# Order of the scores, transposes and gate products in the chunked RWKV pass of a hybrid decoder layer

## The chip, the cores and the metric

The kernel runs on 1 core of one Trainium2 chip. The metric is the device time of one execution in microseconds (us). A core has five engines that work side by side, each through its own queue in order: TensorE (PE: matmuls and transposes; PEld is its weight load), VectorE (DVE), ScalarE (ACT), GpSimd (POOL) and SyncE (SP), the last mostly for DMAs. TensorE writes to PSUM, in banks of up to 128 x 512 fp32 as this kernel uses them.

## The reference, cut to what matters

One layer: an input projection, then an RWKV-7 branch (16 heads of 64) beside an RG-LRU branch, a gated merge, cross-attention and an MLP, for one prompt of 512 rows and 8 single-row samples. The change touches the RWKV scan, which the kernel computes in chunks, and the gates of the RG-LRU:

```
def step(s, inp):                          # RWKV-7, for each row
    r_t, w_t, k_t, v_t, a_t, b_t = inp
    sa = jnp.einsum('bhvk,bhk->bhv', s, a_t)
    s = s * w_t[:, :, None, :] + sa[..., None] * b_t[:, :, None, :] + v_t[..., None] * k_t[:, :, None, :]
    y = jnp.einsum('bhvk,bhk->bhv', s, r_t)
    return s, y
...
gr = jax.nn.sigmoid(jnp.einsum('btnd,nde->btne', blk, W['lru_wa'][l]).reshape(xc.shape) + W['lru_ba'][l])
gi = jax.nn.sigmoid(jnp.einsum('btnd,nde->btne', blk, W['lru_wx'][l]).reshape(xc.shape) + W['lru_bx'][l])
```

## The kernel before, in words

The span begins with weight units: each loads a block of 128 columns of a projection, splits it into a high and a low part (wh by a ScalarE cast, line 95, wl by a VectorE subtraction, line 98), and multiplies it with the split input (xH, xL) into a pair of PSUM banks called mm. adv(n) records the next n units. These matmuls, some 48 a unit, are the filler of everything below.

The RWKV part runs in four passes J = 0 to 3 of two column blocks j = 2J, 2J + 1 (two heads each). For each j, stages E1 to E3 prepare r, k, v, the decays, and the chunk operands: ar (a and r, scaled by the decay up to the row) and bk (b and k, scaled back), eight chunks of 64 rows. Then stage_C1(j) (from line 656) makes

- the scores: 16 products bk x ar, for 8 chunks in two halves, each half into two banks (one a head), which VectorE multiplies with a mask into the tile SC (line 675);
- POOL's scaling of ar (line 678), and a memset of UV (line 682);
- BK: 8 transposes of bk into two banks, copied by ScalarE (line 688);
- UV: 4 transposes of v into one bank, copied by ScalarE (line 693);
- kp (line 697), a product of kp with a matrix of ones, and bv from it (line 701).

Banks: ps1() takes one of two banks (tile ps), psc(s) one of two single banks (tile ch), ps4() changes between both. After the second call stage_C2(J) inverts 32 x 32 triangles of SC on VectorE: two transposes into Am (line 712), a copy Tm, 30 pairs of small steps (tmp line 718, Tm line 720), transposes back (lines 724, 727), and then block products Am x SC and SC x Am on TensorE with ScalarE copies (lines 735, 744). In pass 3 the units of the inverse are mixed with the next work. stage_chain(J) then goes through the eight chunks; each step is a chain of TensorE product, ScalarE copy XS (line 771), product, VectorE copy UV (line 778), product, VectorE update, ScalarE copy y (line 806). Its steps are recorded between the units' matmuls.

gates() (line 541) is recorded behind a unit of the RG-LRU: 4 products of xc with block-diagonal weights bdw (lines 545, 546) into two mm pairs, two tanh each (547, 548), then a chain of activations (552, 553, 559, 560) and VectorE steps.

Around the end of pass 3 three other things are recorded: u_lru loads rows back from DRAM (POOL's DMA rw<-lin_d, line 1078, into two buffers), casts them to xH (ScalarE, line 1080) and xL (VectorE, line 1081); mem_rows transposes the memory tokens (tile mt) and splits them into mh (ScalarE, line 1113) and ml (VectorE, line 1114) for the attention's keys and values; and the u_G units write gate tiles gt (lines 574 to 576).

The order on each engine is drawn by a scheduler from the recorded program. Only a matmul or transpose recorded inside pinned() is tied to stand behind the one recorded before it, without a semaphore.

Of the kernel before, what the change touches and what calls it, by code (L numbers as in the profile page):

```python
# [8 lines left out]
F32 = mybir.dt.float32  # L9
F32R = mybir.dt.float32r  # L10
AF = mybir.ActivationFunctionType
OP = mybir.AluOpType
# [24 lines left out]
def build(tc, d, dbg=None):  # L37
# [43 lines left out]
    def ps4():  # L81

        nr4[0] += 1
        return ps1() if nr4[0] % 2 else psc(nr4[0] // 2 % 2)
# [420 lines left out]
    def u_L(i):  # L505
        def run_y(w):

            p = mm_full(w, X)
            ya, yb = et("ya", pool=LR), et("yb", pool=LR)
            ACT.copy(v2(yb), p[:, :, 0:HA])  # L510
            ACT.copy(SY[:, i, :], p[:, 1, HA:HB])
            ACT.activation(ya, yb, AF.Square, scale=GC)
            DVE.scalar_tensor_tensor(ya, ya, 1.0, yb, op0=OP.add, op1=OP.mult)
            ACT.activation(ya, ya, AF.Tanh, scale=GS)
            DVE.scalar_tensor_tensor(ya, ya, 1.0, yb, op0=OP.add, op1=OP.mult)
            lru[i] = ya
        wunit("w_in", NSH + D + i * 128, run_y)

        def run_u(w):
            ya = lru.pop(i)  # L520
            p = mm_full(w, X)
            ut, bd = ut_[i % 2], bdw[i % 2]
            for n, nm in enumerate(("lru_wa", "lru_wx")):
                for h in range(2):
                    hs = slice(64 * h, 64 * h + 64)
                    SP.dma_start(out=bd[hs, n, hs], in_=d[nm][0, 2 * i + h])
            xt_ = LR.tile([128, T], F32, tag="xc", name="xc")
            xc = xt_[:, 0:S]
            ACT.copy(v2(ut[:, 3:S + 3]), p[:, :, 0:HA])  # L529
            ACT.activation(v2(xc), p[:, :, 0:HA], AF.Identity, scale=par("conv_w", 24 + i),  # L530
                           bias=par("lru_conv_b", i))
            ACT.copy(SU[:, i, :], p[:, 1, HA:HB])
            POOL.tensor_copy(COUT[:, 0, :, i], ut[:, S:S + 3])  # L533
            DVE.tensor_scalar(xt_[:, S:T], SU[:, i, :], par("conv_w", 24 + i), par("lru_conv_b", i),
                              op0=OP.mult, op1=OP.add)
            for jj in range(3):
                cw = par("conv_w", 8 * jj + i)
                DVE.scalar_tensor_tensor(xc, ut[:, jj:jj + S], cw, xc, op0=OP.mult, op1=OP.add)
                DVE.scalar_tensor_tensor(xt_[:, S:T], CB[:, :, jj, i], cw, xt_[:, S:T], op0=OP.mult, op1=OP.add)
            POOL.tensor_copy(SX[:, i, :], xt_[:, S:T])  # L540
            def gates():
                tr, ti = et("tr", pool=LR), et("ti", pool=LR)
                for n, (o, so, bb) in enumerate(((tr, SR, hba), (ti, SI, hbx))):
                    p = mmps()
                    PE.matmul(p[:, 0, 0:HA], bd[:, n, :], xt_[:, 0:HA], start=True, stop=True)
                    PE.matmul(p[:, 1, 0:HB], bd[:, n, :], xt_[:, HA:T], start=True, stop=True)
                    ACT.activation(v2(o), p[:, :, 0:HA], AF.Tanh, scale=0.5, bias=bb[:, i:i + 1])
                    ACT.activation(so[:, i, :], p[:, 1, HA:HB], AF.Tanh, scale=0.5, bias=bb[:, i:i + 1])
                    yield
                DVE.scalar_tensor_tensor(xc, ti, 1.0, xc, op0=OP.add, op1=OP.mult)  # L550
                a0 = et("a0", pool=LR)
                ACT.activation(a0, tr, AF.Exp, scale=c4[:, i:i + 1], bias=c4[:, i:i + 1])
                ACT.activation(tr, tr, AF.Tanh, scale=c4h[:, i:i + 1], bias=c4h[:, i:i + 1])
                yield
                DVE.scalar_tensor_tensor(tr, a0, 1.0, tr, op0=OP.add, op1=OP.mult)
                DVE.tensor_scalar(a0, tr, -1.0, 1.0, op0=OP.mult, op1=OP.add)
                DVE.scalar_tensor_tensor(tr, a0, 1.0, tr, op0=OP.add, op1=OP.mult)
                yield
                ACT.activation(tr, tr, AF.Ln, bias=tiny)
                ACT.activation(tr, tr, AF.Exp, scale=0.5)  # L560
                DVE.scalar_tensor_tensor(xc, xc, 0.5, tr, op0=OP.mult, op1=OP.mult)
                DVE.tensor_tensor_scan(ti, a0, xc, 0.0, op0=OP.mult, op1=OP.add)
                yield
                POOL.tensor_copy(HOUT[:, 0, i:i + 1], ti[:, S - 1:S])
                DVE.scalar_tensor_tensor(ya, ya, 0.5, ti, op0=OP.mult, op1=OP.mult)
                POOL.dma_start(out=lin_d[i], in_=ya)
            later(lambda: side["queue"].append(gates()))
        wunit("w_in", NSH + i * 128, run_u)

# [86 lines left out]
    def stage_C1(j):  # L656
# [5 lines left out]
        SC = CJ["SC"]  # L662
        ar, bk, v = q["ar"], q["bk"], q["v"]
        scv = SC[:, 16 * s:16 * s + 16, :].rearrange("p (c h) n -> p h c n", h=2)
        for half in range(2):
            pp = [ps4(), ps4()]
            for c4_ in range(4):
                c = 4 * half + c4_
                for h in range(2):
# [3 lines left out]
            for h in range(2):  # L673
                p = pp[h]
                DVE.tensor_tensor(scv[:, h, 4 * half:4 * half + 4, :],
                                  p.rearrange("p (c n) -> p c n", c=4),
                                  mask.unsqueeze(1).to_broadcast([128, 4, 128]), op=OP.mult)
        POOL.tensor_tensor(ar[:, 1:NC_].rearrange("p c a t -> p c (a t)"), ar[:, 1:NC_].rearrange("p c a t -> p c (a t)"),
                           q["DL"][:, 0:NC_ - 1].unsqueeze(2).to_broadcast([128, NC_ - 1, 2 * C]), op=OP.mult)
        BK = Cp.tile([128, NC_, 128], F32, tag=f"BK{s}", name="BK")  # L680
        UV = Cp.tile([128, NC_, 128], F32, tag=f"UV{s}", name="UV")
        POOL.memset(UV[0:64], 0.0)
        for half in range(2):
            p = ps1()
            for c4_ in range(4):
                c = 4 * half + c4_
                PE.transpose(p[:, c4_ * 128:(c4_ + 1) * 128], bk[:, c].rearrange("p a t -> p (a t)"), ident)
            ACT.copy(BK[:, 4 * half:4 * half + 4].rearrange("p c n -> p (c n)"), p)
        p = ps1()
        for n in range(4):  # L690
            PE.transpose(p[:, n * 128:(n + 1) * 128], v[:, n * 128:(n + 1) * 128], ident)
        for h in range(2):
            ACT.copy(UV[64:128].rearrange("p (n h) m -> p h n m", h=2)[:, h],
                     p[64 * h:64 * h + 64].rearrange("p (n m) -> p n m", n=4))

        kp = q["kp"]
        DVE.scalar_tensor_tensor(kp, q["r"], par("rw_r_k", j), kp, op0=OP.mult, op1=OP.mult)
        p = ps1()
        PE.matmul(p, bd1, kp, start=True, stop=True)
        bv = et("bv", pool=EO)  # L700
        DVE.tensor_tensor(bv, p, v, op=OP.mult)
        q.update(SC=SC, BK=BK, UV=UV, bv=bv)
# [1268 lines left out]
```

## Time and profile before

| | us |
|---|---|
| median of 3 runs (lowest, highest) | 1376.09 (1371.07, 1384.85) |
| the profiled execution | 1376.98 |
| its span in the trace | 1375.2 |
| TensorE busy | 1295.8 (94%) |
| VectorE busy | 973.4 (71%) |
| ScalarE busy | 622.3 (45%) |
| GpSimd busy | 359.3 (26%) |

The span is from the first to the last instruction; 1.8 us of the execution lie around it. The mean granted TensorE clock over the span is 0.97 of full speed. Matmul ends are modelled, so TensorE's waits are best read from the brackets at the end of a row, which give the idle time before it and what ended it.

### The profile page before, as it was taken

The page shows a single profiled execution, that of the slowest core. Times are in us where ns is not written, and L with a number is a line of the kernel's source. Part 1 is how long each engine was busy: PE and PEld are TensorE (multiplying, and loading weights), DVE is VectorE, ACT ScalarE, POOL GpSimd, SP SyncE. Part 2 cuts the span into 40 slices and gives each one's busy share as a digit, 9 for nine tenths or more (in the row PEclk, how much of TensorE's full clock was granted, in tenths as well). Part 3 has the DMA queues.
Part 4 walks back from the last instruction along what each step waited for, and adds up shares of the span by engine and source line. Part 5 has one row for each costly group of instructions (what it writes and reads, how often), then busy time and mean ns, then how long its engine had stood idle before and what let it go on. Part 6 is the DMA issues. An engine that isn't in the chain of part 4 may idle for free. (4 is left out here: it accounts for less than half of the span.)

```text
span 1375.2 us, 27588 instructions
## 1 busy us (share of the span) xinstructions
PE 1295.8 (94%) x11098; PEld 1202.6 (87%) x11098; DVE 973.4 (71%) x1920; ACT 622.3 (45%) x1199; POOL 359.3 (26%) x423
## 2 busy tenths in 40 slices
PE   7997999999999999888899998998999999999996
PEld 7996988798878887787879998866999999999996
DVE  5578967797679875787855545665667777777755
ACT  4475476537653765443154234442454333333321
POOL 6311000200020012215423124252111444434312
PEclk9999999999999998798999999999999999999998
DMA  7422322221222132474549545784333333333311
GB/s 205 136 73 64 116 60 67 94 82 50 75 91 70 48 93 83 120 210 136 175 138 286 172 115 174 214 267 150 94 91 91 109 93 108 93 92 94 107 64 62
DMA packets 205973, 160.30 MB, mean 117 GB/s; under 512 B 12429, under 2 KB 190911, under 8 KB 205334
## 3 DMA queue, kind: packets, MB, share of 16 engines
q1 hardware_dynamic: 182502, 104.36, 26.1%
q0 software_dynamic: 14592, 47.80, 10.4%
q10 hardware_dynamic: 8752, 6.39, 1.5%
q8 instruction: 87, 1.43, 0.4%
q14 instruction: 40, 0.33, 0.1%
HBM read 137.11 MB, written 21.40 MB: 115 GB/s over the span
## 5 line engine op out<-in xcount | busy, mean ns | idle before, releaser
L47 PE MATMUL mm<-xH,wh 128*128 128x260 f32 (+2 forms) x1824 | 480.0, 292 | 5.9 <-DVE ff L1797 1.7
L47 PE MATMUL mm<-xL,wh 128*128 128x256 f32 (+2 forms) x1824 | 475.2, 289 | 1.0 <-DVE ff L1799 1.0
L47 PE MATMUL mm<-xH,wl 128*128 128x264 f32 (+2 forms) x1568 | 453.8, 290 | 1.2 <-DVE wl L98 1.2
L47 PEld LDWEIGHTS mm<-xH,wh 128*128 128x128 f32 x1824 | 329.9, 191 | 16.5 <-issue 4.3
L47 PEld LDWEIGHTS mm<-xL,wh 128*128 128x128 f32 x1824 | 329.7, 190 | 8.2 <-issue 4.7
L47 PEld LDWEIGHTS mm<-xH,wl 128*128 128x128 f32 x1568 | 298.8, 191 | 8.0 <-issue 4.0
L95 ACT CAST wh<-wr 128x1024 fp32r<-128x1024 f32 x120 | 125.2, 1053 | 178.7 <-PE mm L47 127.0
L47 PE MATMUL mm<-hl,wh 128*128 128x260 f32 (+2 forms) x1056 | 197.0, 285 | 0.9 <-ACT hl L1453 0.9
L98 DVE TENSOR_TENSOR wl<-wr,wh 128x1024 fp32r<-128x1024 f32 x120 | 151.9, 1271 | 56.1 <-ACT wh L95 55.5
L47 PEld LDWEIGHTS mm<-hl,wh 128*128 128x128 f32 x1056 | 163.8, 188 | 2.3 <-ACT hl L1453 1.0
L47 PE MATMUL mm<-hl,wl 128*128 128x260 f32 (+2 forms) x528 | 150.8, 286 | 0.0
L1631 DVE TENSOR_TENSOR wl<-wr,wh 128x512 fp32r<-128x512 f32 x104 | 92.7, 897 | 13.7 <-ACT wh L1630 13.3
L47 PEld LDWEIGHTS mm<-hl,wl 128*128 128x128 f32 x528 | 99.6, 189 | 0.6 <-issue 0.5
L1630 ACT CAST wh<-wr 128x512 fp32r<-128x512 f32 x104 | 62.3, 620 | 53.1 <-PE mm L47 36.4
L47 PE MATMUL mm<-xL,wl 128*128 128x260 f32 (+2 forms) x256 | 72.5, 283 | 0.0
L1799 DVE TENSOR_TENSOR ff<-ff,mm 128x520 f32<-128x520 f32 (+2 forms) x64 | 40.0, 626 | 40.1 <-PE mm L47 40.1
L533 POOL COPY OUTC<-ut 128x3 f32<-128x3 f32 x8 | 2.9, 366 | 193.0 <-ACT ut L529 193.0
L1631 DVE TENSOR_TENSOR wl<-ws,wh 128x512 fp32r<-128x512 f32 x48 | 39.2, 817 | 13.3 <-ACT wh L1630 13.1
L47 PEld LDWEIGHTS mm<-xL,wl 128*128 128x128 f32 x256 | 48.2, 188 | 0.0
L720 DVE TENSOR_TENSOR Tm<-Tm,tmp 64x30 f32<-64x30 f32 (+14 forms) x120 | 40.5, 338 | 3.4
L47 PE MATMUL mm<-mh,wh 128*128 128x256 f32 x128 | 38.8, 305 | 3.7 <-ACT ft L1129 1.8
L794 DVE SCALAR_TENSOR_TENSOR Sbd<-Sbd,DL,ch 64x64 f32<-64x64 f32 x112 | 31.4, 280 | 15.1 <-PE ch L47 12.4
(524 smaller groups left out, 2540.2 us busy)
## 6 DMA issues: line engine op xcount, KB each, us to landing
wr<-in_w_in_dram SPq DMA_DIRECT2D x58, 512.0 KB
wr<-in_mlp_up_dram SPq DMA_DIRECT2D x32, 512.0 KB
wr<-in_mlp_down_dram SPq DMA_DIRECT2D x32, 512.0 KB
vc<-in_cache_mem_v_dram POOLq DMA_DIRECT2D x32, 256.0 KB, 7.3
ff<-in_cache_mem_k_dram POOLq DMA_DIRECT2D x32, 256.0 KB, 4.0
gat_d<-gt POOLq DMA_DIRECT2D x16, 260.0 KB, 2.7
wr<-in_xa_wk_dram SPq DMA_DIRECT2D x8, 512.0 KB
wr<-in_xa_wv_dram SPq DMA_DIRECT2D x8, 512.0 KB
```

The source lines that it names most:

```text
L47: r = nc.tensor.matmul(*a, **k)
L95: a = ACT.copy(h, raw)
L98: DVE.tensor_tensor(l, raw, h.bitcast(F32), op=OP.subtract)
L533: POOL.tensor_copy(COUT[:, 0, :, i], ut[:, S:S + 3])
L720: DVE.tensor_tensor(Tm[:, i + 1:32, 0:i], Tm[:, i + 1:32, 0:i], tv, op=OP.add)
L794: DVE.scalar_tensor_tensor(Sn[s][hs, hs], So[s][hs, hs], Q[s]["DL"][hs, c - 1:c], PX[hs, cs], op0=OP.mult, op1=OP.add)
L1630: pin(ACT.copy(h, src))
L1631: pin(DVE.tensor_tensor(l, src, h.bitcast(F32), op=OP.subtract))
L1799: DVE.tensor_tensor(z, z, p, op=OP.add)
```

## The change

stage_C1 makes UV's memset and kp first. Then, pinned in this order on TensorE: the 8 transposes of bk (ps1, both banks) with the BK copies, the first half of the scores into psc(0) and psc(1), the 4 transposes of v with the UV copies, the product for kp, and the second half of the scores into the same two banks. POOL's scaling of ar and bv follow. The gates' four products are pinned as well. The instructions are the same ones, in number and size.

```diff
                 for n, (o, so, bb) in enumerate(((tr, SR, hba), (ti, SI, hbx))):
                     p = mmps()
-                    PE.matmul(p[:, 0, 0:HA], bd[:, n, :], xt_[:, 0:HA], start=True, stop=True)
-                    PE.matmul(p[:, 1, 0:HB], bd[:, n, :], xt_[:, HA:T], start=True, stop=True)
+                    with pinned():
+                        PE.matmul(p[:, 0, 0:HA], bd[:, n, :], xt_[:, 0:HA], start=True, stop=True)
+                        PE.matmul(p[:, 1, 0:HB], bd[:, n, :], xt_[:, HA:T], start=True, stop=True)
...
-        for half in range(2):
-            pp = [ps4(), ps4()]
+        BK = Cp.tile([128, NC_, 128], F32, tag=f"BK{s}", name="BK")
+        UV = Cp.tile([128, NC_, 128], F32, tag=f"UV{s}", name="UV")
+        POOL.memset(UV[0:64], 0.0)
+
+        kp = q["kp"]
+        DVE.scalar_tensor_tensor(kp, q["r"], par("rw_r_k", j), kp, op0=OP.mult, op1=OP.mult)
+
+        def scores(half):
+            pp = [psc(0), psc(1)]
             for c4_ in range(4):
...
+        with pinned():
+            for half in range(2):
+                p = ps1()
+                for c4_ in range(4):
+                    c = 4 * half + c4_
+                    PE.transpose(p[:, c4_ * 128:(c4_ + 1) * 128], bk[:, c].rearrange("p a t -> p (a t)"), ident)
+                ACT.copy(BK[:, 4 * half:4 * half + 4].rearrange("p c n -> p (c n)"), p)
+            scores(0)
+            p = ps1()
+            for n in range(4):
+                PE.transpose(p[:, n * 128:(n + 1) * 128], v[:, n * 128:(n + 1) * 128], ident)
...
+            p = ps1()
+            PE.matmul(p, bd1, kp, start=True, stop=True)
+            scores(1)
         POOL.tensor_tensor(ar[:, 1:NC_].rearrange("p c a t -> p c (a t)"), ar[:, 1:NC_].rearrange("p c a t -> p c (a t)"),
                            q["DL"][:, 0:NC_ - 1].unsqueeze(2).to_broadcast([128, NC_ - 1, 2 * C]), op=OP.mult)
-        BK = Cp.tile([128, NC_, 128], F32, tag=f"BK{s}", name="BK")
...
```

(The lines removed behind the last one are the same transposes, copies, kp and product in their old place.)

Where the scheduler then puts things is shown at three places. From line 545 on, line numbers of the changed kernel are about one higher, in stage_C1 up to 26 off, and some six higher behind it.

First, TensorE at the first call of stage_C1 in pass 0. Before, from the last scores on (ch and ps are banks, xc,bdw the gates' products, ident,bk the transposes of bk):

```order
L47 MATMUL ch<-ar,bk 128x128
L47 MATMUL ps<-ar,bk 128x128
L47 MATMUL mm<-xc,bdw_277 128x256 x2
L47 MATMUL mm<-xc,bdw_277 128x264 x2
L47 MATMUL mm<-xH,wh 128x256
L47 MATMUL mm<-xL,wh 128x256
L47 MATMUL mm<-xH,wl 128x256
L47 MATMUL mm<-xH,wh 128x256
L52 MATMUL ps<-ident,bk 128x128 x4
```

and in the changed kernel:

```order
L47 MATMUL mm<-xc,bdw_277 128x256
L47 MATMUL mm<-xc,bdw_277 128x264
L47 MATMUL mm<-xc,bdw_277 128x256
L47 MATMUL mm<-xc,bdw_277 128x264
L52 MATMUL ps<-ident,bk 128x128 x8
L47 MATMUL ch<-ar,bk 128x128 x8
L52 MATMUL ps<-ident,v_668 128x128 x4
L47 MATMUL ps<-kp,bd_102 128x512
L47 MATMUL ch<-ar,bk 128x128 x8
L47 MATMUL mm<-xH,wh 128x256
```

The 16 scores have gone from ahead of the gates' products to behind them, and no mm product stands between the parts of stage_C1.

Second, ScalarE at the start of the chain in pass 2 (SC the last block products' copies, XS and y the chain's copies, sq and ic activations of the next pass's decays, ACT_TABLE_LOAD the load of another function table). Before:

```order
L744 COPY SC<-ps 32x16x32 x2
L771 COPY XS<-ch 64x128 x2
L619 ACT_TABLE_LOAD
L619 ACTIVATE sq<-sq 128x512
L609 ACT_TABLE_LOAD
L609 ACTIVATE ic<-mm,ha_231 128x512
L806 COPY y<-ch 128x2x64
L771 COPY XS<-ch 64x128 x2
```

and in the changed kernel:

```order
L777 COPY XS<-ch 64x128 x2
L620 ACT_TABLE_LOAD
L620 ACTIVATE sq<-sq 128x512
L623 ACT_TABLE_LOAD
L623 ACTIVATE sq<-sq 128x512
L812 COPY y<-ch 128x2x64
L620 ACT_TABLE_LOAD
L620 ACTIVATE sq<-sq 128x512
L623 ACT_TABLE_LOAD
L623 ACTIVATE sq<-sq 128x512
L777 COPY XS<-ch 64x128 x2
```

Two more table loads stand between the first XS copies and the second; before, they came later.

Third, VectorE at the second call of stage_C1 in pass 3 (SC the evictions, Am the first step of the inverse, xL and ml the splits). Before:

```order
L1081 TENSOR_TENSOR xL<-rw,xH 128x520 x2
L98 TENSOR_TENSOR wl<-wr,wh 128x1024
L675 TENSOR_TENSOR SC<-ch,mask 128x4x128
L675 TENSOR_TENSOR SC<-ps,mask 128x4x128
L675 TENSOR_TENSOR SC<-ch,mask 128x4x128
L675 TENSOR_TENSOR SC<-ps,mask 128x4x128
L1081 TENSOR_TENSOR xL<-rw,xH 128x520
L712 STREAM_TRANSPOSE Am<-SC 32x1024 x2
L701 TENSOR_TENSOR bv<-ps,v_5824 128x512
L1114 TENSOR_TENSOR ml<-ps,mh 128x512
L713 COPY Tm<-Am 64x1024
```

and in the changed kernel:

```order
L1087 TENSOR_TENSOR xL<-rw,xH 128x520
L98 TENSOR_TENSOR wl<-wr,wh 128x1024
L1087 TENSOR_TENSOR xL<-rw,xH 128x520
L683 TENSOR_TENSOR SC<-ch,mask 128x4x128 x2
L1087 TENSOR_TENSOR xL<-rw,xH 128x520
L707 TENSOR_TENSOR bv<-ps,v_5824 128x512
L1087 TENSOR_TENSOR xL<-rw,xH 128x520
L683 TENSOR_TENSOR SC<-ch,mask 128x4x128 x2
L1120 TENSOR_TENSOR ml<-ps,mh 128x512 x2
L718 STREAM_TRANSPOSE Am<-SC 32x1024
L1120 TENSOR_TENSOR ml<-ps,mh 128x512 x2
L718 STREAM_TRANSPOSE Am<-SC 32x1024
```

The second half's evictions have gone behind the third and fourth xL, and Am behind ml.

## Rows read from the trace of the kernel before

**Rows 1.** The page's first part: busy us, share and count of each engine.

```profile
PE 1295.8 (94%) x11098; PEld 1202.6 (87%) x11098; DVE 973.4 (71%) x1920; ACT 622.3 (45%) x1199; POOL 359.3 (26%) x423
```

**Rows 2.** Windows of the span: length, busy us (count) by engine, clock, DMA share, GB/s.

```profile
core 0: us, PE busy (x) PEld busy (x) DVE busy (x) ACT busy (x) POOL busy (x), PEclk, DMA share, GB/s
...
75.00:135.00 60.00, 51.41 (x403) 46.95 (x404) 50.96 (x82) 39.33 (x65) 12.38 (x15) 0.97 0.26 75
...
220.00:300.00 80.00, 77.50 (x673) 68.08 (x672) 62.98 (x121) 39.69 (x74) 12.61 (x18) 1.00 0.27 86
...
520.00:575.00 55.00, 45.09 (x271) 36.12 (x270) 35.97 (x60) 26.96 (x52) 14.18 (x23) 0.76 0.32 95
575.00:640.00 65.00, 56.66 (x504) 53.74 (x503) 53.03 (x107) 29.17 (x52) 20.45 (x19) 0.89 0.60 175
```

**Rows 3.** Line 675, the scores' evictions: durations in ns, then who waited.

```profile
L675 DVE TENSOR_TENSOR SC<-ps,mask x16: 679/682/686, 109.9 to 560.9; 128x512 f32<-128x512 f32 x16
...
  PE ps L52: 6.7, 5
```

**Rows 4.** Timeline of TensorE, pass 0: start, us, operation, count, [idle before <- releaser].

```profile
101.83 0.37 PE L47 MATMUL ch<-ar,bk 64*128 64x128 f32 x1
...
103.61 0.27 PE L47 MATMUL ps<-ar,bk 64*128 64x128 f32 x1
108.23 3.64 PE L47 MATMUL mm<-xc,bdw 128*128 128x256 f32 x8 [4.35 <-DMA wr<-in_w_in_dram]
112.15 0.39 PE L47 MATMUL mm<-xH,wh 128*128 128x256 f32 x1 [0.29 <-ACT SR L548]
...
126.74 0.66 PE L52 MATMUL ps<-ident,bk 128*128 128x128 f32 x4 [1.70 <-DVE SC L675]
```

**Rows 5.** Timeline of ScalarE, pass 0.

```profile
112.71 0.83 ACT L552 ACTIVATE a<-tr,c 128x512 f32<-128x512 f32 x1
113.42 0.60 ACT L688 COPY BK<-ps 128x512 f32<-128x512 f32 x1
113.88 0.84 ACT L553 ACTIVATE tr<-tr,c4h 128x512 f32<-128x512 f32 x1
```

**Rows 6.** Timeline of TensorE, pass 1, second call.

```profile
272.71 0.66 PE L52 MATMUL ps<-ident,bk 128*128 128x128 f32 x4 [1.49 <-DVE SC L675]
```

**Rows 7.** Timeline of ScalarE, start of the chain in pass 2.

```profile
463.96 0.55 ACT L771 COPY XS<-ch 64x128 f32<-64x128 f32 x2 [0.87 <-PE ch L47]
464.52 1.28 ACT L619 ACT_TABLE_LOAD   x1
465.82 0.63 ACT L619 ACTIVATE sq<-sq 128x512 f32<-128x512 f32 x1
...
468.35 0.26 ACT L806 COPY y<-ch 128x128 f32<-128x128 f32 x1
469.56 0.55 ACT L771 COPY XS<-ch 64x128 f32<-64x128 f32 x2 [0.95 <-PE ch L47]
```

**Rows 8.** Timeline of TensorE, pass 3.

```profile
560.46 0.66 PE L52 MATMUL ps<-ident,bk 128*128 128x128 f32 x4 [1.49 <-DVE SC L675]
...
566.25 1.11 PE L52 MATMUL ps<-ident,v 128*128 128x128 f32 x4 [3.89 <-ACT BK L688]
...
625.54 2.60 PE L47 MATMUL ps<-Am,SC 32*32 32x32 f32 x64 [3.73 <-DVE Am L724]
```

**Rows 9.** Timeline of ScalarE, pass 3, second call.

```profile
565.09 0.63 ACT L1080 CAST xH<-rw 128x520 fp32r<-128x520 f32 x1 [3.38 <-DMA rw<-lin_d]
```

**Rows 10.** Timeline of VectorE, pass 3, second call.

```profile
557.98 1.23 DVE L98 TENSOR_TENSOR wl<-wr,wh 128x1024 fp32r<-128x1024 f32 x1
...
562.62 3.81 DVE L712 STREAM_TRANSPOSE Am<-SC 32x1024 f32<-32x1024 f32 x2
...
577.49 0.20 DVE L720 TENSOR_TENSOR Tm<-Tm,tmp 64x30 f32<-64x30 f32 x1
```

**Rows 11.** Tile rw: the DMAs that fill it, from issue to landing.

```profile
DMA to landing us min/median/max: 2.9/3.2/5.8
```

More of the change, by code (lines that the diff above doesn't have):

```diff
@@ L677, in stage_C1 @@
                                   mask.unsqueeze(1).to_broadcast([128, 4, 128]), op=OP.mult)
+        with pinned():
[9 more added lines that the diff above has]
+                PE.transpose(p[:, n * 128:(n + 1) * 128], v[:, n * 128:(n + 1) * 128], ident)
+            for h in range(2):
+                ACT.copy(UV[64:128].rearrange("p (n h) m -> p h n m", h=2)[:, h],
+                         p[64 * h:64 * h + 64].rearrange("p (n m) -> p n m", n=4))
+            p = ps1()
+            PE.matmul(p, bd1, kp, start=True, stop=True)
+            scores(1)
         POOL.tensor_tensor(ar[:, 1:NC_].rearrange("p c a t -> p c (a t)"), ar[:, 1:NC_].rearrange("p c a t -> p c (a t)"),
                            q["DL"][:, 0:NC_ - 1].unsqueeze(2).to_broadcast([128, NC_ - 1, 2 * C]), op=OP.mult)
-        BK = Cp.tile([128, NC_, 128], F32, tag=f"BK{s}", name="BK")
[L681 to L699, printed above, removed]
         bv = et("bv", pool=EO)
```

## The prediction

> **What bounds the kernel now.** I read the page's busy shares first [rows 1]: TensorE is busy for 94% of the span and no other engine for more than 71%, so outside a few places every microsecond that TensorE does not wait is a microsecond won. Then I cut the span into stages [rows 2]. The change touches only the four passes of the chunked RWKV part, from about 100 to 570 us. In the first (75 to 135 us) TensorE is busy 51.4 of 60 us, in the last (520 to 575) 45.1 of 55 at a mean granted clock of 0.76. In the stage of pass 1's second call (220 to 300) it is busy 77.5 of 80. So the waits to be won lie at the two ends.
>
> Third, who waits for the masked evictions of the scores [rows 3]: TensorE's matmuls do 5 times, 6.7 us together, always the transposes of bk, which need a bank that still holds scores. That is the wait the change is made of: four banks are filled with scores, and the next user waits for VectorE, which needs 0.68 us for each.
>
> Fourth, the order listing. No instruction is added or removed; the change is the order, and of that the part that the scheduler draws itself once the products are pinned. I take four places.
>
> **A, pass 0.** In the first call of stage_C1 the 16 scores run from 101.83 to 103.72, and then TensorE stands still until the gates' products at 108.23 [rows 4]. The scores fill the beginning of a hole that is there anyway. Now the gates' products are pinned ahead of all of stage_C1 (first order listing), so the scores and transposes come after 108.23, where the hole can't hide them: +1.9 us, as long as the scores are.
>
> Behind the gates (end 108.23 + 3.64 = 111.87) come 8 transposes, at 0.11 us each like the scores about 0.9, and half the scores, 0.95: 113.7. The v transposes need the first of ps1's two banks back, which the first BK copy frees. That copy ran from 113.42 to 114.0; ScalarE now does the second tanh of the decay first, 0.84 us [rows 5], so 114.9: a wait of 1.2. The second half of the scores waits for both evictions of the first, on a VectorE that stands among the gates' own steps; the trace does not show this wait, and I bound it by 0 and the two evictions, 1.3, and take the middle, 0.6, since the v transposes and the product for kp cover about half. Small waits of before go (0.29 ahead of 112.15, and the changes of shape between mm and transposes, some 0.2). Sum of the first call: 1.9 + 1.2 + 0.6 - 0.5 = +3.2.
>
> In the second call the 1.70 before 126.74 [rows 4] goes; a wait of 0.5 comes for the first half's evictions, which the order puts behind a weight subtraction of 1.23 [rows 10]: -1.2. A = +2.0, between 0 and +4.
>
> **B, passes 1 and 2.** Each second call has the same wait of 1.49 [rows 6], one of the five of [rows 3], with 0.15 for the change of engine state around it. With the new order a free ScalarE and VectorE cover everything: the first BK copy (0.6) runs under four transposes and eight scores, the evictions under v's transposes and the kp product. Each engine has other work in its queue, so I give 0.4 back: -1.2 per pass; B = -2.4, between -3.3 (all of it) and 0 (two evictions late, 1.3, in each).
>
> **C, start of the chain in pass 2.** The chain's ScalarE step is the copy XS. Before, between two steps stand two table loads, two activations and y, and XS comes at 469.56 after an idle 0.95 [rows 7]. In the new order there stand four table loads, four square-root/exponential activations and y (second order listing): 4 x 1.28 + 4 x 0.63 + 0.26 = 7.9 us after 464.51, that is 472.4, 2.8 later. TensorE has 22 large matmuls between the two steps by the order, 23 before, so nothing more covers it. C = +2.8; below by 0, if the two pairs are done before the first XS is free, above by +4 with VectorE's answer late as well.
>
> The price of a table load is worth a second look. The row says 1.28, and the activation behind it starts 0.02 after its end [rows 7]. The Trainium skill (ScalarE: Activation LUTs, section "What ACT_TABLE_LOAD costs") gives 1283 ns for the load and about 1380 ns of drain for each switch. By that rule the two extra loads would cost 2.8 us more and the sum below would be 1382.4; the trace agrees with the load and shows no drain here.
>
> **D, pass 3.** Here the change looks best on TensorE: it removes a 1.49 for evictions, and above all the 3.89 before the v transposes at 566.25 [rows 8], which waited for BK copies that stood behind an xH cast waiting for its DMA [rows 9]. ScalarE now copies BK before that cast. But the stage's end is VectorE's: TensorE waits 3.73 at 625.54 for the transposed inverse [rows 8], which ends a chain of small VectorE steps that begins with Am at 562.62 [rows 10]. TensorE being 5.4 earlier makes that wait longer and nothing else. What counts is when the inverse's first update comes, 577.49 before. In the new order (third listing) the second half's evictions stand behind four xL, and the fourth needs the cast, the cast a DMA, the DMA the buffer freed by the second xL, now itself behind the weight subtraction: xL ends at 559.8, the DMA issued right behind it lands 5.8 later, the longest of the eight (3.2 is the median [rows 11]), about 565.7; cast and xL 567.0, two evictions 568.2. Between and behind the two Am (1.9 each) stand four ml, whose mh casts the order puts behind xH five and six, so behind two more landings; the last ml ends at about 573.3, the second Am at 575.2, Tm, a weight subtraction and xL about 3.4: 578.6. D = +1.1; -1.5 if the landing takes 3.2, +5 if two more are late.
>
> **Sum.** 2.0 - 2.4 + 2.8 + 1.1 = +3.5 on the profiled execution's own 1376.98 (span 1375.2 and 1.8 around it): 1380.5. That execution lies 0.9 above the median of the runs shown, 1376.09, so 1379.6. From 740 us on the orders are equal, and nothing there changes. All terms at their low ends give 1376.09 + 0 - 3.3 + 0 - 1.5 = 1371.3, at their high ends 1389.1.
>
> **Rivals.** First, the waits go and are not given back: A's new waits vanish under the small steps, C's table loads are done early, and pass 3 was bound by TensorE's low clock rather than by VectorE. For it: TensorE is the bound everywhere else, and at 0.76 of the clock, of two levels 1.2 and 2.4 GHz, about 0.48 of 55 us was at the lower one. Against: the wait for Am at 625.54. It gives 6.7 of [rows 3], 3.9 of [rows 8] less the 1.9 of A: 1376.09 - 8.7 = 1367.4; with 0.48 x 45.1 us of work, half of it back, up to 10.8 more, 1356.6. Chance 0.18, 0.07 of it below -1%.
>
> Second, slower: pass 3's inverse starts much too late. Place: the ml and evictions behind xL on VectorE. Price: each further landing at 5.8 instead of 3.2 adds 2.6 [rows 11]; three make +7.8. TensorE then idles before Am, and if the stage 575 to 640 (0.89) falls to the 0.76 of the one before, 0.26 more of its 56.7 us of work is done at half speed, +7.4. With the sum: 1379.6 + 15.2 = 1394.8. It decides the sign beyond 1% once the first update comes later than about 583 us. For it: three queues now wait in a ring through buffers of two. Against: the median landing is 3.2. Chance 0.13.
>
> Third, the change does not do what it says: each wait is only exchanged for one of the same size, 1376 to 1377. For it: order alone moves, and ScalarE and VectorE do the same work at the same places. Chance 0.15. Fourth, ScalarE stops behind a table load for as long as the load takes, 1.28: with two more loads between the steps +2.6, 1382.2; against it the row, where 0.02 lie between load and activation [rows 7]. Chance 0.02. (The drain that the Trainium skill names, above, would be such a stop.)
>
> **How the numbers follow.** My forecast, a small loss inside the noise, has 0.52. A measurement of this kernel can tell about 1% (13.8 us) from no change; its own three runs lie 13.8 apart. Forecast, third, fourth and most of the first are within it; faster 0.07, slower 0.13, same 0.80. For the range I go from the first rival's time without the clock's gift, 1367, nearly to the slower one, 1392; below lie 0.08, above 0.11.
>
> **What would show it.** A: in the changed trace TensorE idle from about 101.7 to 108.2, scores after 112, and a wait of 1 to 2 us before the v transposes for a BK copy. B: no wait of 1.5 before the second calls' transposes. C: an XS copy of the chain in pass 2 more than 7 us after the one before, with TensorE idle 2 to 3 us. D: the wait for Am near 625 longer than 3.7, by about what pass 3 saves. I am wrong if that wait shrinks, if the chain's XS is on time, or if a stage that the change does not touch moves by more than a microsecond.

## The result, and the profile after

The changed kernel takes 1383.21 us (median of 18 runs, 1378.05 to 1385.87), the kernel before 1375.39 beside it (18 runs, 1364.34 to 1386.10): a ratio of 1.0057, with a 95% interval of 1.0037 to 1.0076. It is slower by about 7.8 us, inside the 1% that the prediction counts as no change, and inside its range. The profiled execution took 1385.69, of which the span is 1384.0. Executions of the kernel before spread by some 20 us: of 133, here and in the rounds of the experiments, 39 took over 1380 (granted clock mostly 0.96 to 0.97), of the 72 of experiments 7 to 12 none, so a ratio depends in part on how many of them its rounds hold; one execution of 3 (3071.39) and one of 5 (1754.21) are left out of the medians below.

The page's first part, which answers to [rows 1]:

```profile
span 1384.0 us, 27592 instructions
...
PE 1296.5 (94%) x11098; PEld 1199.2 (87%) x11098; DVE 970.3 (70%) x1920; ACT 621.2 (45%) x1199; POOL 358.9 (26%) x423
```

The counts of each engine are those of before (four more of 27592 instructions are none that the page counts as busy), and TensorE's busy time is the same to within 0.7 us. The difference is in its idle time: 1384.0 - 1296.5 = 87.5 us, where before it was 1375.2 - 1295.8 = 79.4.

The windows of [rows 2], with the same columns (length, busy us and count of PE, PEld, DVE, ACT and POOL, clock, DMA share, GB/s), and one more over the chain of pass 2:

```profile
75.00:135.00 60.00, 52.12 (x401) 47.30 (x400) 47.97 (x77) 40.43 (x69) 12.44 (x14) 0.94 0.25 75
220.00:300.00 80.00, 77.87 (x684) 67.70 (x685) 62.62 (x120) 38.33 (x75) 13.53 (x19) 1.00 0.29 87
400.00:520.00 120.00, 111.29 (x1062) 98.88 (x1060) 93.86 (x187) 61.81 (x116) 11.03 (x15) 0.94 0.23 68
520.00:575.00 55.00, 45.28 (x356) 35.83 (x352) 37.79 (x75) 32.81 (x65) 15.78 (x26) 0.94 0.35 110
575.00:640.00 65.00, 52.77 (x419) 50.92 (x420) 54.62 (x108) 25.84 (x44) 13.33 (x14) 0.87 0.53 150
```

The stage of pass 1 is a little fuller (77.9 against 77.5). From the chain of pass 2 on the windows no longer cover the same work, since everything runs later: the last XS copy of that chain starts at 530.75 here (row below) and at 520.98 before. So places are compared by instructions, not by windows.

TensorE's timeline at the four places (the lines between are left out):

```profile
108.95 3.80 PE L47 MATMUL mm<-xc,bdw 128*128 128x256 f32 x8 [4.89 <-ACT gt L576]
112.54 1.71 PE L52 MATMUL ps<-ident,bk 128*128 128x128 f32 x8
114.19 1.16 PE L47 MATMUL ch<-ar,bk 64*128 64x128 f32 x16
115.28 0.66 PE L52 MATMUL ps<-ident,v 128*128 128x128 f32 x4
115.77 1.02 PE L47 MATMUL ps<-kp,bd 128*128 128x512 f32 x2
116.73 1.58 PE L47 MATMUL ch<-ar,bk 64*128 64x128 f32 x16
...
125.81 1.09 PE L52 MATMUL ps<-ident,bk 128*128 128x128 f32 x8 [1.57 <-DVE bk L641]
...
271.95 1.06 PE L52 MATMUL ps<-ident,bk 128*128 128x128 f32 x8 [0.65 <-DVE bk L641]
...
477.64 0.33 PE L47 MATMUL ch<-XS,SC 64*64 64x64 f32 x2 [2.66 <-ACT XS L777]
...
634.45 1.77 PE L47 MATMUL ps<-Am,SC 32*32 32x32 f32 x30 [4.79 <-DVE Am L730]
```

In pass 0 the scores are exposed, as forecast: they run from 114.19, behind the gates' products. The waits for evictions of [rows 4, 6, 8] are gone; in their place stand a wait of 1.57 for bk itself in pass 0 and of 0.65 in pass 1 (in pass 2 as well, at 414.79). The v transposes, at 115.28 and in pass 3, wait for nothing. The chain of pass 2 waits 2.66 for XS, and the wait for the inverse has grown from 3.73 to 4.79.

ScalarE, at the start of pass 2's chain and in pass 3:

```profile
468.83 0.55 ACT L777 COPY XS<-ch 64x128 f32<-64x128 f32 x2 [0.34 <-PE ch L47]
469.40 1.28 ACT L620 ACT_TABLE_LOAD   x1
470.69 0.63 ACT L620 ACTIVATE sq<-sq 128x512 f32<-128x512 f32 x1
471.34 1.28 ACT L623 ACT_TABLE_LOAD   x1
...
476.81 0.63 ACT L623 ACTIVATE sq<-sq 128x512 f32<-128x512 f32 x1
477.35 0.53 ACT L777 COPY XS<-ch 64x128 f32<-64x128 f32 x2
...
530.75 0.55 ACT L777 COPY XS<-ch 64x128 f32<-64x128 f32 x2 [0.53 <-PE ch L47]
...
568.34 0.62 ACT L1086 CAST xH<-rw 128x520 fp32r<-128x520 f32 x1 [2.54 <-DMA rw<-lin_d]
...
572.15 0.62 ACT L1086 CAST xH<-rw 128x520 fp32r<-128x520 f32 x1 [1.99 <-DMA rw<-lin_d]
```

Two XS pairs of the chain now start 477.35 - 468.83 = 8.52 us apart, 5.60 before [rows 7]; four table loads fill the space. In pass 3 two xH casts hold ScalarE until their rows have landed.

VectorE, in pass 0 (one row, used further down) and in pass 3:

```profile
106.20 0.28 DVE L534 TENSOR_SCALAR xc<-SU,PT 128x8 f32<-128x8 f32 x1
...
566.25 1.29 DVE L683 TENSOR_TENSOR SC<-ch,mask 128x512 f32<-128x512 f32 x2
...
568.99 0.70 DVE L1087 TENSOR_TENSOR xL<-rw,xH 128x520 fp32r<-128x520 f32 x1 [1.46 <-ACT xH L1086]
...
572.81 0.70 DVE L1087 TENSOR_TENSOR xL<-rw,xH 128x520 fp32r<-128x520 f32 x1 [2.51 <-ACT xH L1086]
573.42 1.28 DVE L683 TENSOR_TENSOR SC<-ch,mask 128x512 f32<-128x512 f32 x2
...
579.13 2.04 DVE L718 STREAM_TRANSPOSE Am<-SC 32x1024 f32<-32x1024 f32 x1
...
584.27 0.20 DVE L726 TENSOR_TENSOR Tm<-Tm,tmp 64x30 f32<-64x30 f32 x1
...
628.29 0.18 DVE L726 TENSOR_TENSOR Tm<-Tm,tmp 64x30 f32<-64x30 f32 x1
631.70 0.69 DVE L987 TENSOR_REDUCE mst<-sp 128x8 f32<-128x512 f32 x1 [3.23 <-POOL sp L982]
632.30 2.00 DVE L730 STREAM_TRANSPOSE Am<-Tm 32x1024 f32<-32x1024 f32 x1
```

The reader is to see two places where VectorE stands still with the inverse ready to go on: ahead of the second half's evictions it waits 1.46 and 2.51 for xH, and behind the last update (628.29) a reduction of another piece of work, mst, waits 3.23 for POOL, with the transposes back queued behind it.

One caution on single profiles. A second profiled execution of the changed kernel (in the run repeated below) took 1376.0, 9.7 less than the first. Of this 2.4 lie in the first loads, and 5.6 between the 85th and the 115th weight unit (738 to 989 us in the kernel before), where the two orders are the same. So the prediction's last sign of being wrong, an untouched stage that moves by more than a microsecond, also shows between two executions of one kernel. Rows are therefore read for who waits for whom, and verdicts are taken from the timed rounds.

### The profile page after: what moved, and what is told of

The parts are those of the page before. It is cut to its first block, busy times and chain, and to the rows that moved or that the text cites. A ratio compares the mean times of both kernels' runs of the same rounds, so it can differ in the third digit from the quotient of the medians.

```text
span 1384.0 us, 27592 instructions
## 1 busy us (share of the span) xinstructions
PE 1296.5 (94%) x11098; PEld 1199.2 (87%) x11098; DVE 970.3 (70%) x1920; ACT 621.2 (45%) x1199; POOL 358.9 (26%) x423
## 5 line engine op out<-in xcount | busy, mean ns | idle before, releaser
L98 DVE TENSOR_TENSOR wl<-wr,wh 128x1024 fp32r<-128x1024 f32 x120 | 147.4, 1235 | 60.0 <-ACT wh L95 59.4
L47 PE MATMUL mm<-mh,wl 128*128 128x256 f32 x128 | 39.3, 309 | 4.5 <-DVE wl L98 4.5
```

The lines of the kernel that those rows point to most:

```text
L47: r = nc.tensor.matmul(*a, **k)
L98: DVE.tensor_tensor(l, raw, h.bitcast(F32), op=OP.subtract)
```

## The experiments

The expectations speak of theories. By the first (T1) the loss comes from the four table loads at the start of pass 2's chain, by the second (T2) from pass 3, by the others (T3, T4) from pass 0: its exposed scores and pinned gates, or a lower clock at its block products. "New" and "old" below mean stage_C1 in the changed or the former order; a pass is chosen by

```diff
+    def stage_C1(j):
+        (stage_C1_new if j // 2 in (...) else stage_C1_old)(j)
```

Each ratio is to the kernel before on the same chip, with its 95% interval. Where two ratios are compared, the interval of the difference is worked out from theirs.

**1. Fewer table loads at the start of pass 2's chain.** The changed kernel, with the logarithms of both column blocks side by side in the preparation of pass 3.

```diff
-        for q in Q:
-            ACT.activation(q["sq"], q["sq"], AF.Ln, scale=65536.0)
+        pin = tc.keep_in_program_order if J == 3 else (lambda i: i)
+        ACT.activation(Q[0]["sq"], Q[0]["sq"], AF.Ln, scale=65536.0)
+        pin(ACT.activation(Q[1]["sq"], Q[1]["sq"], AF.Ln, scale=65536.0))
+        if J == 3:
+            pin(ACT.activation(Q[0]["sq"], Q[0]["sq"], AF.Exp, scale=-0.5))
...
```

> The changed kernel, with one thing undone: in the stage that prepares pass 3 the two Ln activations stand side by side on ScalarE, and the first Exp right behind them (tied in program order), so two table loads instead of four stand between the first and the second XS copies of the chain in pass 2. Theory T1 (the loss is made at the chain's start in pass 2: XS comes some 3 us late behind the loads, and TensorE then runs at the lower clock): 1383.2 less 2.6 of loads and less most of the 5 to 6 of clock, so about 1376 (1374 to 1379), with no wait over 1 us for XS there and a granted clock of 1.00 from 478 to 492. Rival T2 (the loss is pass 3's inverse, late on VectorE): 1383 (1381 to 1385). Rival T3 (the loss is pass 0, where the scores lost their hole): also 1383.

Measured: 1379.58, ratio 1.0033 (1.0005 to 1.0060). By the ratios 1.4 to 3.3 us less than the changed kernel; the intervals overlap, and most of the loss stays. The wait for XS is down to 0.95 in the profile, but the granted clock from 478 to 492 is 0.76 there and not 1.00.

**2. Old order in pass 2 alone** (new in 0, 1 and 3).

```diff
+        (stage_C1_new if j // 2 in (0, 1, 3) else stage_C1_old)(j)
```

> The changed kernel with the old stage_C1 in pass 2 alone; passes 0, 1 and 3 and the gates as changed. The order listing has the old run of table loads at the chain's start in pass 2 (two between the first XS copies and the second). T1: the loss goes, 0.8 of the gain of pass 2's own second call is given back: 1374 to 1377. T2 and T3: 1382 to 1385.

Measured: 1381.64, 1.0032 (1.0005 to 1.0059). Again most of the loss is left without pass 2's change.

**3. New order in pass 2 alone**, the gates not pinned.

```diff
+        (stage_C1_new if j // 2 in (2,) else stage_C1_old)(j)
```

> The kernel before with the new stage_C1 in pass 2 alone, the gates' products not pinned. The order listing shows the four table loads between XS copies. T1: 1375.4 + 8 - 1 = 1382 to 1384, with a wait of 2 to 3 us for XS and 13 us at the lower clock behind it. T2 and T3: 1374 to 1375, since pass 2 gains the 1.5 of its eviction wait and nothing else moves.

Measured: 1376.53, 1.0008 (0.9976 to 1.0039), although the chain waits exactly as in the changed kernel (TensorE's timeline):

```profile
475.84 0.32 PE L47 MATMUL ch<-XS,SC 64*64 64x64 f32 x2 [2.66 <-ACT XS L827]
```

The granted clock from 478 to 492 is 0.91 here. Pass 2 alone costs nothing that shows, though its interval reaches 5 us, and T1 as the whole cause falls. That the gain at the evictions pays for the wait at the chain is read from the rows.

**4. New order in pass 3 alone**, the gates not pinned.

```diff
+        (stage_C1_new if j // 2 in (3,) else stage_C1_old)(j)
```

> The kernel before with the new stage_C1 in pass 3 alone, the gates' products not pinned. T1, with the traces' landmarks (the changed kernel is 11 us behind at 540 us and 9 behind at the wait for the inverse near 630): pass 3 gains about 2, 1372 to 1375. T2: it loses 5 to 8: 1380 to 1384. My prediction's term D: +1, 1376.5.

Measured: 1378.97, 1.0044 (1.0018 to 1.0070): alone it costs most of what the whole change costs, 6.1 us by the ratio. By the medians beside each other (1376.27 before) it is 2.7.

**5. New order in pass 0 alone**, with the gates pinned.

```diff
+        (stage_C1_new if j // 2 in (0,) else stage_C1_old)(j)
```

> The kernel before with the new stage_C1 in pass 0 alone and the gates' products pinned; behind the start of pass 0's chain the order is that of before. Four runs have left 4 to 5 us of the loss outside pass 2. Theory T4 (pass 0's new order lets the granted clock fall at the block products before its chain, as in the traces of two of the three runs with that order, 10 us at half and 5 lost): 1376 + 0.3 + 4 to 5 in most executions, median 1379 to 1381, and the fall is in the profile between 170 and 185 us. Rival T2 (the rest of the loss is pass 3): 1376 to 1377.

Measured: 1375.78, 0.9999 (0.9966 to 1.0033). Alone, pass 0 and the gates show no cost, though the interval reaches 4.5 us. The granted clock from 174 to 182 is 1.00 in this profile, so T4's fall is not there; 6 and 7 come back to it.

**6. The changed kernel once more**, without an edit, beside 5, 7 and 8.

> The changed kernel once more, beside the others on one chip: 1383 (1381 to 1385). If T1 and T4 both hold, this second profile shows the lower clock at one or both of two places: near 175 us, or behind the wait for XS near 478.

Measured: 1382.83, 1.0043 (1.0020 to 1.0065). The loss is there again, and T4's fall too: the granted clock from 174 to 182 is 0.50. Behind the wait for XS it hardly fell.

**7. New order in passes 1, 2 and 3**, the gates not pinned, the logarithms side by side as in 1.

```diff
+        (stage_C1_new if j // 2 in (1, 2, 3) else stage_C1_old)(j)
```

> The changed kernel with pass 0 as before and the gates not pinned, and with the two Ln activations ahead of the chain in pass 2 kept side by side (passes 1, 2, 3 new). T1 and T4 together: pass 0 costs nothing, pass 2's chain starts with two table loads instead of four, passes 1 and 2 keep their gain of about 1.7 each, so 1372 to 1376, no slower than before. T2: pass 3 is the loss and stays: 1379 to 1382.

Measured: 1376.24, 0.9992 (0.9969 to 1.0015), hardly above what T1 and T4 expect and below T2. This kernel differs from that of 1 in nothing but pass 0 and the gates, and it takes 0.41% less (0.05 to 0.77), 5.6 us; by the medians 3.3. So with the other passes new, pass 0's new order does cost time, which 5 alone did not show.

**8. The same without pass 3.**

```diff
+        (stage_C1_new if j // 2 in (1, 2) else stage_C1_old)(j)
```

> As the run before it, with pass 3 old too (only passes 1 and 2 new, Ln side by side). Beside that run it gives pass 3 alone. T1 and T4: 1 to 2 us slower than it or the same, 1373 to 1377. T2: 4 to 6 us faster than it, 1373 to 1375.

Measured: 1370.20, 0.9961 (0.9939 to 0.9984): faster than the kernel before. With the logarithms paired, the chain's XS pairs start 7.05 us apart instead of 8.52, and TensorE's timeline shows a shorter wait:

```profile
473.82 0.33 PE L47 MATMUL ch<-XS,SC 64*64 64x64 f32 x2 [0.96 <-ACT XS L831]
```

Between 7 and 8 lie 1376.24 - 1370.20 = 6.0 us by the medians and 0.31% (4.3 us) by the ratios, for pass 3 alone, in line with 4. The views of VectorE's waits in pass 3 (engine, line, releaser: us in total, times, longest) show what differs; the waits of wl for its casts, 4 to 5 us in both, are left out. In 7:

```profile
DVE xL L1141 <- ACT xH L1140: 4.4, 2, 2.5
DVE mst L1041 <- POOL sp L1036: 4.3, 1, 4.3
```

and in 8, up to the end of the inverse:

```profile
DVE xL L1141 <- ACT xH L1140: 0.5, 1, 0.5
```

Two waits of about 4 us each are new ahead of the inverse's end: for xH ahead of Am, and for POOL's sp behind the last update. (8 waits 4.5 for sp as well, but only behind the transposes back.) In 8 these follow the last update at once (VectorE's timeline):

```profile
619.13 0.18 DVE L780 TENSOR_TENSOR Tm<-Tm,tmp 64x30 f32<-64x30 f32 x1
619.35 2.05 DVE L784 STREAM_TRANSPOSE Am<-Tm 32x1024 f32<-32x1024 f32 x1
```

**9. As 7, with xL from the third on tied behind the second Am.**

```diff
-            DVE.transpose(out=Am[sl], in_=SC[sl, :, sl].rearrange("p h t -> p t h"))
+            CJ["am"] = DVE.transpose(out=Am[sl], in_=SC[sl, :, sl].rearrange("p h t -> p t h")).ins
...
+                    with tc.issue_after(CJ["am"]) if k >= 2 else ExitStack():
-                    DVE.tensor_tensor(xL[:, k, :], t, xH[:, k, :].bitcast(F32), op=OP.subtract)
+                        DVE.tensor_tensor(xL[:, k, :], t, xH[:, k, :].bitcast(F32), op=OP.subtract)
```

> The kernel of e7 (passes 1, 2, 3 new, Ln side by side) with one edge more: on VectorE the third and later xL stand behind the second Am of pass 3, so the second half's evictions and the first Am no longer wait behind two xL. Theory T2' (pass 3's loss is the start of the inverse, late behind the DMA-fed xL): Am starts 1 to 3 us earlier, the inverse is done 2 to 4 us earlier, median 1372 to 1374 instead of 1376.2. Rival (the loss is elsewhere, say in the two ml pairs around Am and the order of the casts): no gain, 1375 to 1378.

Measured: 1374.24, 0.9994 (0.9974 to 1.0014): no gain. VectorE's wait has only changed its name:

```profile
DVE ml L1175 <- ACT mh L1174: 3.4, 1, 3.4
```

ml needs the mh casts, and these stand on ScalarE behind the xH casts that wait for the same DMAs.

**10. The same tie with the old order in pass 3** (as 8 otherwise).

> The same edge in the kernel of e8 (passes 1 and 2 new, pass 3 old). There one xL stands between the evictions and Am, 0.7 us, and two in the inverse's first steps move by a step: T2' expects 0 to 2 us gained, 1368 to 1371; the rival no difference, 1370.

Measured: 1371.12, 0.9957 (0.9931 to 0.9984), as 8. Against 9 it is a third measure of pass 3's price: 3.1 us by the medians, 0.37% (5.1 us) by the ratios.

**11. As 8, without the pairing of the logarithms.**

```diff
-        pin(ACT.activation(Q[1]["sq"], Q[1]["sq"], AF.Ln, scale=65536.0))
...
+        for q in Q:
+            ACT.activation(q["sq"], q["sq"], AF.Ln, scale=65536.0)
```

> The kernel of e8 without the Ln pairing: passes 1 and 2 new, four table loads between the first XS copies of pass 2's chain as in the changed kernel. T1 in its smaller form (the wait for XS costs 1.6 to 2.9, and the clock falls behind it in some executions only): 1372.5 to 1375 against e8's 1370.2, with the wait of 2.9 for XS back in the trace. If the loads cost nothing: 1370.

Measured: 1374.82, 0.9994 (0.9969 to 1.0018). The wait of 2.66 for XS is back in the profile. Against 8 the two extra table loads at the chain cost 0.33% (0.00 to 0.66), 4.6 us by the medians. That is about what the new order in passes 1 and 2 gains in 8.

**12. As 9, with the xH casts from the third on tied behind the four mh casts as well**, so that nothing that waits for those DMAs stands ahead of Am on either engine.

```diff
-            ACT.copy(h, p)
+            CJ["mh"] = ACT.copy(h, p).ins
...
+                    with tc.issue_after(CJ["mh"]) if k >= 2 else ExitStack():
-                    ACT.copy(xH[:, k, :], t)
+                        ACT.copy(xH[:, k, :], t)
```

> The kernel of e9 (passes 1, 2, 3 new, Ln side by side, third and later xL behind Am on VectorE) with the same on ScalarE: the third and later xH casts stand behind the four mh casts. e9 only moved the wait, from xL waiting for xH to ml waiting for mh, which stand behind the same DMA-fed casts on ScalarE. If that ring is pass 3's loss (T2''), then VectorE no longer idles for xH or mh ahead of the second Am, which ends 3 to 5 us earlier than in e7 (44 to 47 us behind the last XS of pass 2's chain instead of 50), and the median is 1370 to 1373. Rival (what is lost in pass 3 is set behind Am, by the weight splits' and the sample steps' share of VectorE, and starting earlier buys nothing): the second Am ends earlier, the inverse does not, 1374 to 1377.

Measured: 1368.93 (1365.17 to 1373.16), ratio 0.9932 (0.9905 to 0.9960): the fastest median of the study, faster than both kernels. The ratio flatters it, since the kernel before took 1379.70 in these rounds, against 1374 to 1376 beside the others; by the medians it is 7.3 us below 7, and 1.3 and 2.2 below 8 and 10, from which its interval does not tell it apart. The waits for xH and mh are gone (VectorE's waits in pass 3, the two longest):

```profile
DVE wl L98 <- ACT wh L95: 6.0, 4, 3.9
DVE mst L1041 <- POOL sp L1036: 3.7, 1, 3.7
```

The second Am ends 45.2 us behind the start of pass 2's last XS pair, against 48.5 in 9. But the inverse is not done earlier than in 7: its transposes back start 102.0 us behind that pair, against 102.3 in 7 and 106.0 in 9. What 9 and 12 have over 7 lies behind it: the chain of pass 3 takes 53.4 and 53.5 us from its first XS to its last, against 60.2 in 7. In 9 the late inverse gives most of this back, in 12 not: the first XS of that chain comes 116.9 us behind the pair in 7, 121.6 in 9 and 115.6 in 12. So neither expectation had the whole mechanism. In both VectorE did two more weight subtractions ahead of the inverse's end, 12 instead of 10; that the chain is shorter because of them is argued, not shown. Both ties with the old order in pass 3 were not run, so how much of 12's gain belongs to pass 3's new order stays open.

## Why the prediction came out as it did

The time was forecast at 1379.6, a loss of 3.5; measured were 7.8 (1.0057) and 6 (1.0043). The verdict, the sign and the range hold. By its own steps:

| step | forecast, us | measured, us | from |
|---|---|---|---|
| A, pass 0 and gates | +2.0 | -0.1 (-4.7 to +4.5); +5.6 (+0.7 to +10.6) | 5; 1 against 7 |
| B and C, passes 1 and 2 | -2.4 + 2.8 = +0.4 | -0.8 (-4.3 to +2.5) | 11 |
| of it the extra table loads (C) | +2.8 | +4.6 (0 to +9.1), and +1.4 to +3.3 | 11 against 8; changed kernel against 1 |
| D, pass 3 | +1.1 | +6.1 (+2.5 to +9.6); +4.3 (-0.1 to +8.7); +5.1 (+0.6 to +9.7) | 4; 7 against 8; 9 against 10 |
| sum | +3.5 | +5.2 | 5, 11 and 4 |

(Ratios times the median before, some 1376.) The three parts measured alone add up to 5.2, the whole was measured at 6 and 7.8. Each part is known to 3.5 or 5 us only, so this does not show that the parts simply add; A's two measures differ by 5.7.

**A was wrong in its parts, and its size stays open.** Both measures allow +2.0. That the scores would be exposed is right, and the idle time ahead of the gates' products is there (4.89). The steps that failed are the two waits of the first call, "a wait of 1.2" before the v transposes and 0.6 before the second half of the scores, which no row shows; and the second call waits 1.57 for bk, not 0.5 for evictions.

The prediction also lacked a lower clock, which is theory T4. In all five profiles with the new order in pass 0 TensorE waits 0.6 us for r (line 447) between 171 and 174; in none of the nine others. Behind this wait the granted clock is 0.50, the lower of its two levels, from 174 to 182 in three of the five (1, 2 and 6), and 1.00 in the first profile of the changed kernel, in 5 and in the nine others. The rows are TensorE's of 6, then the windows of 6 and of the first profile:

```profile
171.38 0.36 PE L47 MATMUL mm<-xH,wh 128*128 128x256 f32 x1 [0.63 <-DVE r L447]
...
174.00:182.00 8.00, 8.00 (x83) 6.56 (x84) 0.69 (x1) 2.27 (x5) 0.00 (x0) 0.50 0.22 64
174.00:182.00 8.00, 8.00 (x111) 7.13 (x111) 2.10 (x3) 3.56 (x6) 0.00 (x0) 1.00 0.48 133
```

From VectorE's step at line 534 (rows below) to the first XS copy of pass 0's chain lie 76.7 to 77.0 us in these three, 73.3 and 73.4 in the other two. How many of the timed executions have the fall is not known.

Against the exposed scores stands a gain that was not in the prediction either. Before, POOL's scaling of ar began just as VectorE started a small step on the way to the gates (one row of VectorE, one of POOL):

```profile
104.03 1.73 DVE L534 TENSOR_SCALAR xc<-SU,PT 128x8 f32<-128x8 f32 x1
```

```profile
104.06 1.68 POOL L678 TENSOR_TENSOR ar<-ar,DL 128x896 f32<-128x896 f32 x1 [0.65 <-issue]
```

In the changed kernel that scaling comes 14 us later, and the same VectorE step takes 0.28 at 106.20 (row above): 1.45 us won on the path to the gates, whose products start 2.75 us behind that step's start, before 4.20.

```profile
118.45 1.97 POOL L704 TENSOR_TENSOR ar<-ar,DL 128x896 f32<-128x896 f32 x1 [8.72 <-issue]
```

All nine profiles with the old order in pass 0 show 1.73 for it, all five with the new order 0.28 or 0.29.

**B was right in kind:** the 1.49 became 0.65, where "0.4 back" was allowed for. No run measures it without the table loads but 8, where the two passes, with the logarithms paired, gain 5.4 us (2.2 to 8.4), more than the 2.4 forecast.

**C was right,** and its price of 2.8 lies among those measured, 1.4 to 4.6. (The four activations are logarithms and exponentials; none is the square root that the prediction names.) The copy was forecast 7.9 us behind the end of the one before; it came 7.97 behind (477.35 - 468.83 - 0.55), and TensorE waited 2.66 of the forecast 2 to 3. In the changed kernel's own profile the granted clock also fell behind that wait (windows):

```profile
478.00:492.00 14.00, 13.22 (x98) 10.56 (x98) 5.90 (x15) 3.60 (x9) 0.00 (x0) 0.54 0.24 77
```

The second profile of the same kernel has the same wait of 2.66 at 478.12 and hardly that fall:

```profile
478.00:492.00 14.00, 12.62 (x127) 10.42 (x128) 6.60 (x16) 6.16 (x16) 0.00 (x0) 0.88 0.25 77
```

From the second XS pair to the last of the chain the first took 2.0 us longer than before, the second 1.4 less. How often the clock falls there, and so whether this is why the loads cost 4.6 and not 2.8, stays open. The rule of a drain with each table load, which the Trainium skill gives (ScalarE: Activation LUTs, "What ACT_TABLE_LOAD costs", about 1380 ns), is not borne out: four loads stand in the row here, and the activation at 470.69 starts 0.01 behind the end of the load before it (469.40 + 1.28), the load at 471.34 0.02 behind the activation.

**D is the term that was too small,** by 3 to 5 us. The prediction's reading of the order was right: evictions and Am behind xL, xL behind a cast, the cast behind a DMA. Behind the last XS pair of pass 2 (530.75) the second Am ends 579.13 + 2.04 - 530.75 = 50.4 us; before, with the pair at 520.98 (ScalarE's timeline, below) and Am ending at 562.62 + 3.81 [rows 10], 45.5.

```profile
520.98 0.55 ACT L771 COPY XS<-ch 64x128 f32<-64x128 f32 x2 [0.53 <-PE ch L47]
```

Over all profiles it is 49.7 to 50.7 in the six with the plain new order in pass 3, 45.5 to 48.3 in the six with the old one (10 among them). Two steps failed. The first: the inverse's first update at 577.49 was taken as what the old order does. By that yardstick pass 3 gained 3 us (53.5 against 56.5), so that D has the right sign is luck. It is 56.5 us behind the XS pair, but in the six profiles with the old order it lies anywhere between 51.0 and 56.5. Before, VectorE waited 3.1 us for mh in that stage (the view of its waits):

```profile
DVE ml L1114 <- ACT mh L1113: 3.1, 4, 1.7
```

This wait and TensorE's 3.89 for BK [rows 8] are not always there: in 5 and 8 both are absent, and the update comes at 51.0 us. The new order gives 52.8 to 54.2 each time. The forecast compared it with one of the late executions. The second: the prediction stopped at the first update. At the other end of the inverse the new order puts the reduction mst, with its wait of 3.23 for POOL, ahead of the transposes back; in the old order that wait falls behind them (before at 632.55, with the transposes back from 623.38 on; in 8 likewise). In 12 a wait of 3.7 stays ahead of them and the kernel is the fastest all the same, so this wait can be no more than a part of the price. The forecast "wait for Am near 625 longer than 3.7" is right (4.79), but "by about what pass 3 saves" is not: pass 3 saved nothing.

What is shown: pass 3's new order costs 4 to 6 us by the ratios of three pairs, 3 to 6 by their medians, and with the DMA-fed casts and subtractions tied behind the inverse's start the kernel is faster than before (12). The share of the mst wait was not tried by itself. What stays open: from the XS pair to the first XS of the next chain the profiles of the new order take 114.4 to 117.1 us, of the old 109.2 to 117.3; the means, 115.9 and 113.6, differ by 2.3, so about half of the price is seen in that stage. In the two profiles shown above it is 117.1 and 116.7: this pair alone would not have shown the loss.

**The rivals.** The first (waits go and aren't given back) would have been right for passes 1 and 2 with the loads paired: 8 is 0.39% faster. The second named the right place and the right ring of waits, and too high a price: two waits of 4.0 us together for xH instead of 7.8, and hardly a lower clock behind them (0.87 in the last window, 0.89 before). The third fits pass 0 alone (5), and not pass 0 beside the other passes (1 against 7). The fourth fell with the rows at 469.40 to 471.34.

## What to carry to other kernels

When an order is pinned on one engine, read what the scheduler then does with the queues of the others: here an in-order VectorE and ScalarE got work that waits for a DMA or for POOL ahead of the one chain that the next stage needs, and tying that work behind the chain was worth 7.3 us by the medians (12 against 7), as much as the 6.7 of waits that the change set out to remove. Before comparing a forecast with one row of before, see in more than one execution whether that wait is always there. Try a change that touches four places at each place alone, and also take each place out of the whole: here pass 3 cost time both ways, but pass 0 cost nothing alone and some 3 to 6 us beside the others, where a short wait was followed by a lower clock in three profiles of five.

## What the runs showed of the hardware

A VectorE step beside a GpSimd one can last as long as that one: the 128 x 8 step took 1.73 us beside a scaling of 1.68, and 0.28 or 0.29 without it. It ended at 104.03 + 1.73 = 105.76, 0.02 behind GpSimd's 104.06 + 1.68 = 105.74. The Trainium skill (SBUF — State Buffer, section "SBUF: two separate sides") says that the two engines share a pair of ports, which one holds for a whole instruction while the other stands still. The length agrees with that; that whichever starts first gets the pair does not show, since VectorE's row begins 0.03 earlier and is yet the one that waits.

A wait of TensorE of the same length does not always end in a lower clock: behind one of 0.56 to 0.63 us the granted clock was 0.50 from 174 to 182 in three profiles and 1.00 in two.
